# Two mixer blocks on one core: other places where the mixers' generators yield, other step rates, and another machine model in the scheduler

## The chip, the cores and the metric

The kernel runs on one core of a Trainium2 chip. The core has a matrix engine (TensorE, PE in the profile, with its weight loads shown apart as PEld), VectorE (DVE), ScalarE (ACT), GpSimd (POOL) and SyncE (SP), which here only issues transfers. The metric is the device time of one execution in microseconds (us), the median of three runs. PE's granted clock is given as a share of full speed: 1.00 is 2.4 GHz, 0.50 is 1.2 GHz.

## The reference

The input is `x` of 1024 tokens by 1024 features, in 32-bit floats. Two blocks follow one another.

```python
# first block (16 meta tokens stand in front of x)
proj = h @ w_in
y_a = hgrn2_mixer(q, f, i, g, ...)       # chunked linear attention with forget gates, 6 heads of 64
y_b = mamba2_mixer(z, xbc, dt, ...)      # convolution of 4 taps, state space scan, 6 heads, norm
y_c = s5_mixer(u, ...)                   # diagonal complex state space, gelu, then y * sigmoid(y @ glu_w + glu_b)
mixed = concatenate([y_a, y_b, y_c]) @ w_out
h = layer_norm(ALPHA * h + mixed)
h = layer_norm(ALPHA * h + square(relu(h @ w_mlp_in)) @ w_mlp_out)
...
# second block, in outline
qkv, z, beta, a, uv, gates = split(h @ w2)
y_1 = deltanet_branch(qkv, z, beta, a, ...)   # gated delta rule: a triangular inverse for each chunk, 4 heads of 128
y_2 = spatial_gating_branch(uv, ...)          # layer norm, a masked product over 128 tokens, a gate
h = layer_norm(ALPHA * h + (gated sum of y_1 and y_2, each projected) @ w_o)
h = layer_norm(ALPHA * h + conv_ffn(h))
```

## The kernel before

The tokens go through in two halves of 512. Work is of two kinds. **Dense** work is products with weights of the model: `weights` loads a block of 512 KB (tile `wr`, on SP's queue), ScalarE rounds it to the high part `wh`, VectorE subtracts for the low part `wl`, and `mm3` adds three matmuls (high by high, high by low, low by high) into PSUM tiles named `ps`. Operands (`xt`, or `f` where they come out of the mixers' tiles) are split in the same way. **Mixer** work is everything between a projection and the next one: small matmuls and transposes into PSUM tiles named `px`, with ScalarE and VectorE making the operands of the next matmul. Both pools have four banks.

A mixer is a Python generator that yields between pieces (steps). `steps`, called `st` in `run`, advances the dense generator and, after each of its steps, the mixer by `r` steps; `both` advances generators in turns. So the program's order is a mesh of the two kinds. From it the framework's scheduler makes the order of each engine: it takes the instructions by their place in the program, as its model of the machine says that they become ready. The engines then run their own orders one by one, and a waiting instruction holds up all behind it.

In `run` the stages are: the first projection `p1` with S5, HGRN2 and Mamba2 of the first half beside it; the gate of S5 (`glu`, two products of 128x512 tiles into `px`); `out_proj` of the first half and the MLP, with the second half's mixers beside them; the second block's projection `p2` for the first half and the MLP of the second half, with `mix2(0)` (delta rule for four heads, two at a time, then the spatial gating) beside them; the merge (`merge`) and `out_proj`; `p2` and the first half's FFN with `mix2(1)`; then merge, `out_proj` and FFN of the second half.

What a mixer hands on goes through DRAM: `Y1[h]` and `Y2[h]` are written by POOL's queue, read back by SP's (`load_y`: tile `ev`) and split into `xt` or `f`. In Mamba the steps' cumulative sums `m2dA` are a matmul's operand; their rows are stored to DRAM (`rows`) and come back for every chunk spread over all partitions, in two loads that ScalarE's queue issues:

```python
for c in range(c0, 5):
    ...
    for g in range(2):
        nc.scalar.dma_start(W[g][:, :, :L], rows[i:i + 3, :L]...)
        self.act(eA[g][:, :, :L], W[g][:, :, :L], AF.Exp)
```

The spatial gating ends each block of 128 tokens with four transposes (line 1175), a copy and a store to `Y2`. In the delta rule the inverse doubles its diagonal blocks: twelve small matmuls, a ScalarE copy into `Z`, matmuls on `Z`.

## Time and profile before

| | |
|---|---|
| three runs | 2838.29, 2840.65, 2842.82 us; median 2840.65 |
| span of the profiled execution | 2831.3 us |
| the median lies above that span by | 9.35 us |
| busy share of PE, weight loads, VectorE, ScalarE, GpSimd | 98, 80, 63, 41, 8% |

The profile comes from one execution. The span runs from its first to its last recorded instruction, so what lies around it (launch and end) is not in it. Times in the rows are from the span's start. A matmul's end is modelled, so "busy" counts a little more than work. Idle time in square brackets is the time in which the engine stood before the instruction, with what released it.

### The profile page before, as it was taken

The numbers are of one execution on the slowest core, as the hardware profiler recorded it, in microseconds if no ns is written. First come the engines' busy times: TensorE is split into PE (matmuls) and PEld (weight loads), VectorE is DVE, ScalarE is ACT, GpSimd is POOL, SyncE is SP. The second block draws the span as 40 slices with busy tenths as digits, with TensorE's granted clock in tenths as the row PEclk, the third lists the DMA queues.
The fourth block names the chain that finished last, engine by engine and source line by source line (L and its number), as shares of the span: only waits on it lengthen the run. The fifth ranks groups of instructions, "written<-read, shape, count | busy, mean of one in ns | idle before, by whom it ended". The sixth has DMA issues, their size and how long they took to land.

```text
span 2831.3 us, 37337 instructions
## 1 busy us (share of the span) xinstructions
PE 2768.6 (98%) x14176; PEld 2262.4 (80%) x14176; DVE 1793.7 (63%) x3321; ACT 1163.4 (41%) x1810; POOL 220.4 (8%) x365
## 2 busy tenths in 40 slices
PE   8999999999999999999999999999999999999997
PEld 7788777777878878877788888888788888888886
DVE  7678768777756554386545675535867557675556
ACT  4334344444442353364323334435545334344432
POOL 3121000000001121010000001110100000000000
PEclk9999999999999999999999999999999999999999
DMA  7333462323344444333333455433244433342232
GB/s 220 122 94 93 139 202 81 113 89 113 106 147 149 157 144 133 123 101 123 105 104 119 142 184 166 126 126 130 79 136 140 149 104 101 107 139 92 97 96 75
DMA packets 138036, 351.55 MB, mean 124 GB/s; under 512 B 26779, under 2 KB 40641, under 8 KB 137857
## 3 DMA queue, kind: packets, MB, share of 16 engines
q1 hardware_dynamic: 113712, 295.34, 32.9%
q0 software_dynamic: 16672, 48.50, 5.0%
q10 hardware_dynamic: 7473, 5.34, 0.7%
q8 instruction: 111, 1.82, 0.3%
q14 instruction: 68, 0.56, 0.1%
HBM read 296.84 MB, written 51.69 MB: 123 GB/s over the span
## 4 chain that ended last, share of the span: by engine, by line
PE 81%; issue 7%; DVE 6%; DMA 2%; ACT 2%; POOL 1%; SPq 0%; DVEq 0%; POOLq 0%; ACTq 0%
PE ps L204 73%; PE px L204 7%; DVE f L192 2%; ACT f L189 1%; DVE wl L192 1%; PE px L1265 1%; DVE f L195 1%; DMA hx<-ev 1%; DMA wr<-in_w 0%; DVE acc L195 0%; DMA f<-rows 0%; DVE f L433 0%; ACT wh L189 0%; DVE ta L192 0%; ACT ev L189 0%
## 5 line engine op out<-in xcount | busy, mean ns | idle before, releaser
L204 PE MATMUL ps<-xt,wh 128*128 128x512 f32 (+1 forms) x3616 | 1117.0, 388 | 8.7 <-ACT wh L189 8.5
L192 DVE TENSOR_TENSOR wl<-wr,wh 128x1024 fp32r<-128x1024 f32 (+3 forms) x431 | 521.5, 1210 | 606.7 <-ACT wh L189 590.2
L189 ACT ACTIVATE wh<-wr 128x1024 fp32r<-128x1024 f32 (+3 forms) x431 | 452.3, 1050 | 898.4 <-PE ps L204 826.1
L204 PE MATMUL ps<-wh,xt 128*128 128x512 f32 (+3 forms) x2624 | 813.1, 384 | 4.7 <-ACT xt L189 4.4
L204 PEld LDWEIGHTS ps<-xt,wh 128*128 128x128 f32 x3616 | 665.9, 189 | 141.7 <-ACT wh L189 8.5
L204 PE MATMUL ps<-xt,wl 128*128 128x512 f32 (+1 forms) x1808 | 698.6, 387 | 3.9 <-DVE wl L192 3.9
L204 PEld LDWEIGHTS ps<-wh,xt 128*128 128x128 f32 (+1 forms) x2624 | 485.8, 188 | 99.9 <-ACT xt L189 6.9
L204 PE MATMUL ps<-wl,xt 128*128 128x512 f32 (+3 forms) x1312 | 502.2, 383 | 0.8 <-DVE wl L192 0.7
L204 PEld LDWEIGHTS ps<-xt,wl 128*128 128x128 f32 x1808 | 341.5, 189 | 72.8 <-DVE wl L192 5.5
L204 PE MATMUL ps<-f,wh 128*128 128x512 f32 x960 | 300.5, 394 | 0.0
L204 PEld LDWEIGHTS ps<-wl,xt 128*128 128x128 f32 (+1 forms) x1312 | 246.7, 188 | 46.5 <-DVE wl L192 2.0
L189 ACT ACTIVATE f<-f 128x512 f32<-128x512 f32 (+6 forms) x300 | 178.5, 613 | 200.6 <-DVE f L192 62.3
L204 PE MATMUL px<-f,f 128*128 128x128 f32 (+8 forms) x1832 | 201.4, 258 | 16.8 <-DVE f L192 10.2
L204 PEld LDWEIGHTS ps<-f,wh 128*128 128x128 f32 x960 | 180.3, 188 | 42.3
L189 ACT ACTIVATE ev<-ps 128x512 f32<-128x512 f32 (+4 forms) x303 | 169.6, 561 | 72.9 <-PE ps L204 67.1
L192 DVE TENSOR_TENSOR acc<-acc,ps 128x512 f32<-128x512 f32 x192 | 130.8, 683 | 95.8 <-PE ps L204 93.9
L204 PE MATMUL ps<-f,wl 128*128 128x512 f32 x480 | 189.4, 394 | 0.0
L204 PEld LDWEIGHTS px<-f,f 128*128 128x128 f32 (+2 forms) x1192 | 133.3, 180 | 52.9 <-issue 22.8
L192 DVE TENSOR_TENSOR f<-f,f 128x256 f32<-128x256 f32 (+5 forms) x244 | 128.6, 547 | 39.0 <-ACT f L189 37.0
L189 ACT ACTIVATE xt<-ev 128x512 fp32r<-128x512 f32 x131 | 82.3, 629 | 149.2 <-DVE ev L192 145.9
L195 DVE SCALAR_TENSOR_TENSOR ev<-ev,p,ev 128x512 f32<-128x512 f32 x176 | 132.2, 751 | 2.7 <-ACT ev L189 0.6
L192 DVE TENSOR_TENSOR xt<-ev,xt 128x512 fp32r<-128x512 f32 x124 | 85.9, 696 | 49.6 <-ACT xt L189 49.1
(223 smaller groups left out, 2046.9 us busy)
## 6 DMA issues: line engine op xcount, KB each, us to landing
wr<-in_w SPq DMA_DIRECT2D x93, 512.0 KB, 3.8
wr<-in_wup SPq DMA_DIRECT2D x88, 512.0 KB, 3.5
wr<-in_wmi SPq DMA_DIRECT2D x64, 512.0 KB, 3.6
wr<-in_wmo SPq DMA_DIRECT2D x64, 512.0 KB, 3.6
wr<-in_wdn SPq DMA_DIRECT2D x44, 512.0 KB, 3.5
wr<-in_wo SPq DMA_DIRECT2D x32, 512.0 KB, 3.7
Y<-f POOLq DMA_DIRECT2D x32, 256.0 KB, 2.6
ev<-Y SPq DMA_DIRECT2D x32, 256.0 KB, 3.6
```

The costliest lines, as they stand in the source:

```text
L189: self.nc.scalar.activation(out=out, in_=in_, func=func, **kw)
L192: self.nc.vector.tensor_tensor(out=out, in0=a, in1=b, op=op)
L195: self.nc.vector.scalar_tensor_tensor(out=out, in0=a, scalar=s, in1=b, op0=op0, op1=op1)
L204: self.nc.tensor.matmul(out, lhsT, rhs, start=start, stop=stop)
L1265: nc.tensor.transpose(b[:, 128 * t:128 * t + 128], acc[t][:, 128 * k:128 * k + 128], self.ident)
```

## The change

Three things are changed, and no arithmetic. First, `yield`s are added or moved in the five mixers, so that a step begins with matmuls and ends with making the next operands: in HGRN2 between the operands of a level and its matmuls, in the delta rule after each copy or product that the next matmul reads, and squares are computed before the yield in front of their sums. In HGRN2 the diagonal scores move from the level of block size 1 to the first level. Second, the rates `r` in `run` rise, as the mixers now have more steps. Third, the framework is told to order the program by its other machine model (`schedule_with_timeline_sim`). Comments and docstrings are taken out as well, which shifts line numbers by some 6 to 16.

```diff
@@ -425,6 +425,7 @@
...
                     self.tt(y4[o:o + 64, :, hd, :].rearrange("p c (n b) -> p c n b", b=b), c5(M, o), c5(q, o), ALU.mult)
+                yield
                 ps = self.bank()
@@ -438,13 +439,12 @@
...
                         self.act(S[j:j + b, :, j + b:j + 2 * b], ps[j:j + b, :, j + b:j + 2 * b])
+                yield
                 scores(M, M, b, put)
-            yield
-            if b == 1:
+            if i == 0:
                 di = self.mask(M_ID)
                 scores(q, kr, 0, lambda S, ps: nc.vector.copy_predicated(out=S, mask=di, data=ps))
-        yield
@@ -457,24 +457,27 @@
...
+        yield
...
         self.act(kT, b)
-        dS = self.bank().rearrange("p (c d) -> p c d", d=64)
         if h == 0:
...
             self.act(kTm[:16], b[:16, :128])
+        yield
+        dS = self.bank().rearrange("p (c d) -> p c d", d=64)
+        if h == 0:
             for o in (0, 64):
@@ -488,19 +491,21 @@
...
         self.hs[p] = last
+        yield
         o_ = self.bank()
...
                 self.mm(o_[o:o + 64, t:t + 128], v[:, c, o:o + 64], ST[hd][:, c, :], False, True)
-        yield
...
         self.act(g, g, AF.Silu)
+        sq = self.square(o_)
+        yield
         ms = self.bank()
-        self.sums(ms, [(self.blk, self.square(o_), slice(0, 128))])
+        self.sums(ms, [(self.blk, sq, slice(0, 128))])
         r = self.t(528)[:, :512]
@@ -584,6 +589,7 @@
...
                 self.m2a.rearrange("p (o h) -> p o h", o=1).to_broadcast([128, 5 - c0, 6]), ALU.mult)
+        yield
         b = self.bank()
@@ -666,6 +672,7 @@
...
             sq.append(self.square(Y[j]))
+        yield
         ones, left, right = self.ones, self.band[:, 128:256], self.band[:, 0:128]
@@ -934,6 +941,7 @@
...
             self.act(y[j], y[j], AF.Gelu_apprx_tanh)
+        yield
         for m in range(2):
@@ -990,22 +998,23 @@
...
             self.conv4(self.S2["qkv", j, h][:, 0:515], 512, P_CWQ + 4 * j, None, x)
+        sq = [self.square(x) for x in (q, k)]
         yield
-        for x, bias in ((q, self.lnq), (k, 0.0)):
+        for x, y, bias in ((q, sq[0], self.lnq), (k, sq[1], 0.0)):
             b = self.bank()
-            self.sums(b, [(self.ones, self.square(x), slice(0, 128))])
+            self.sums(b, [(self.ones, y, slice(0, 128))])
             r = self.t(512)
...
             self.tt(x, x, r, mult)
-        yield
         E, eR = self.t(512), self.t(512)
...
+        yield
@@ -1016,8 +1025,7 @@
...
         self.act(vt, b)
-        yield
@@ -1059,6 +1067,7 @@
...
             self.act(self.halves(Z, 0, lb), nb(b))
+            yield
             b = self.bank()
@@ -1079,13 +1088,14 @@
...
             self.stt(c3(R16), c3(b), 1024.0, k1024, mult, add)
+            yield
             b = self.bank()
@@ -1098,9 +1108,11 @@
...
                 self.tt(R, vt[:, s], b[:, 0:128], sub)
+                yield
             b = self.bank()
...
             self.act(u, b[:, 0:128], AF.Copy, scale=col(be, c))
+            yield
             if S is not None:
@@ -1116,8 +1128,10 @@
...
         self.act(z, z, AF.Silu)
+        sq = self.square(o)
+        yield
         b = self.bank()
-        self.sums(b, [(self.ones, self.square(o), slice(0, 128))])
+        self.sums(b, [(self.ones, sq, slice(0, 128))])
         r = self.t(512)
@@ -1164,21 +1178,22 @@
...
             self.stt(v, v, rs, lb, ALU.mult, ALU.add)
+            yield
             b = self.bank()
...
                 self.stt(u[:, s], b[:, s], self.col(P_BS + g), u[:, s], ALU.add, ALU.mult)
+            yield
             b = self.bank()
...
                                 v.rearrange("p (g t) -> p g t", g=4))
-            yield
@@ -1485,25 +1500,25 @@
...
         m = self.both(m, self.seq(0))
-        st(p1, 3, m, 2.7)
-        st(p1, 10, m, 3)
-        st(p1, 99, m, 3, False)
+        st(p1, 3, m, 3.1)
+        st(p1, 10, m, 3.5)
+        st(p1, 99, m, 3.5, False)
         st(m)
...
         m = self.mix1(1)
-        st(self.out_proj(ys, ap["wo1"], a0), 99, m, 0.75, False)
+        st(self.out_proj(ys, ap["wo1"], a0), 99, m, 0.9, False)
         x0 = []
...
         st(n)
-        st(q, 76, m, 0.6, False)
+        st(q, 76, m, 0.72, False)
         st(m)
@@ -1514,11 +1529,11 @@
...
         st(n)
-        st(p, 99, m, 0.6, False)
+        st(p, 99, m, 1.15, False)
         q = self.mlp(x1, a1)
-        st(q, 80, m, 0.8, False)
+        st(q, 80, m, 1.5, False)
         st(m)
@@ -1531,9 +1546,9 @@
...
         st(n)
-        st(p, 99, m, 0.6, False)
+        st(p, 99, m, 1.15, False)
         q = self.ffn(0, x0, a0, ((0, 4), (4, 4), (8, 4), (12, 4), (16, 4), (20, 2)))
-        st(q, 36, m, 1, False)
+        st(q, 36, m, 1.9, False)
         st(m)
@@ -1706,7 +1721,7 @@
...
     args["out"] = nc.dram_tensor("out_0", (1024, 1024), F32, kind="ExternalOutput").ap()
-    with tile.TileContext(nc) as tc:
+    with tile.TileContext(nc, schedule_with_timeline_sim=True) as tc:
         body(tc, **args)
```

The engines' orders follow from all three together. Three places show it, all on PE.

The first is the start of Mamba's chunk loop for the first half. In the order of before, the matmuls on `m2dA` stand among dense rows of the first projection (`ps_3463`), and so do the first transposes of a chunk (L624, L633).

```order
L204 MATMUL px_3416<-m2dA_3414,o 128x30
L204 MATMUL px_3420<-o,m2dA_3414 30x128
L204 MATMUL ps_3463<-xt_119,wh_3458 128x512 x2
L624 MATMUL px_3444<-c,f_3083 16x128
L624 MATMUL px_3444<-c,f_3084 16x128
L624 MATMUL px_3444<-c,f_3085 16x128
L633 MATMUL px_3452<-c,f_3086 16x128
L204 MATMUL ps_3463<-xt_119,wl_3459 128x512
L204 MATMUL ps_3463<-xt_124,wh_3458 128x512 x2
L204 MATMUL ps_3463<-xt_124,wl_3459 128x512
L204 MATMUL ps_3463<-xt_129,wh_3458 128x512 x2
```

In the new order, the last dense rows, those of `out_proj` (`ps_4341` to `ps_4344`), are followed by the same chunk loop (L630 and L639 are its transposes there, `m2S` its state).

```order
L204 MATMUL ps_4344<-wl_4378,xt_4313 128x512
L204 MATMUL ps_4341<-wh_4377,xt_4313 128x512
L204 MATMUL ps_4342<-wh_4377,xt_4313 128x512
L204 MATMUL ps_4343<-wh_4377,xt_4313 128x512
L204 MATMUL ps_4344<-wh_4377,xt_4313 128x512
L204 MATMUL px_3598<-f_3592,f_3585 128x192 x2
L204 MATMUL px_3624<-f_3283,f_3281 128x128
L204 MATMUL px_3624<-f_3284,f_3282 128x128
L630 MATMUL px_3634<-c,f_3278 128x128
L630 MATMUL px_3634<-c,f_3279 128x128
L630 MATMUL px_3634<-c,f_3280 128x128
L639 MATMUL px_3642<-c,f_3281 128x128
```

What moved: the chunks came between the first projection's dense rows; now the dense rows stand ahead of them, and from the first of these `px` rows to the two products of `glu` there is no `ps` row.

The second place is a doubling of the delta rule's inverse in the second half (the 128x64 rows; the LDWEIGHTS rows are their operands). Before, the group `px_17546` reads what ScalarE makes of `px_17540`.

```order
L204 MATMUL px_17540<-f_17481,f_17482 128x64
L204 MATMUL ps_17653<-wl_17500,xt_17073 128x512
L204 MATMUL ps_17653<-wh_17499,xt_17073 128x512
L204 MATMUL ps_17653<-wh_17505,xt_17208 128x512
L204 LDWEIGHTS f_17482
L204 MATMUL px_17546<-f_17481,f_17482 128x64
```

In the new order the same kind of step reads as follows; `px_17454` belongs to the other head of the pair, and the group that reads what ScalarE makes of `px_17448` stands 15 rows behind this piece.

```order
L204 MATMUL px_17448<-f_17216,f_17217 128x64
L204 MATMUL ps_17659<-wh_17607,xt_17328 128x512
L204 MATMUL ps_17659<-wh_17607,xt_17445 128x512
L204 MATMUL ps_17659<-wl_17608,xt_17445 128x512
L204 MATMUL ps_17659<-wh_17607,xt_17445 128x512
L204 MATMUL ps_17707<-wh_17601,xt_17014 128x512
L204 MATMUL ps_17707<-wl_17602,xt_17014 128x512
L204 MATMUL ps_17707<-wh_17601,xt_17014 128x512
L204 MATMUL ps_17707<-wh_17601,xt_17143 128x512
L204 MATMUL ps_17707<-wl_17602,xt_17143 128x512
L204 MATMUL ps_17707<-wh_17601,xt_17143 128x512
L204 LDWEIGHTS f_17233
```

What moved: between a group and the one that depends on it there were three dense rows, and now there are seventeen, and the other head's group.

The third place is the end of the spatial gating of the second half (transposes L1175, in the new listing L1191). Before, they stand among the dense rows of the FFN.

```order
L1175 MATMUL px_18575<-c,f_18552 128x128
L204 MATMUL ps_18655<-xt_14951,wh_18651 128x512
L1175 MATMUL px_18575<-c,f_18552 128x128
L204 MATMUL ps_18655<-xt_14951,wl_18652 128x512
L1175 MATMUL px_18575<-c,f_18552 128x128
L204 MATMUL ps_18655<-xt_14959,wh_18651 128x512 x2
L204 MATMUL ps_18655<-xt_14959,wl_18652 128x512
L204 MATMUL ps_18655<-xt_14967,wh_18651 128x512 x2
L204 MATMUL ps_18655<-xt_14967,wl_18652 128x512
```

In the new order they are followed by the merge: `ps_19138`, `ps_19152` and `ps_19182` are its tiles, `f_19090` the first operand that the spatial gating gives.

```order
L204 MATMUL ps_19138<-f_19084,wh_19128 128x512
L204 MATMUL ps_19138<-f_19085,wh_19128 128x512
L204 MATMUL ps_19138<-f_19084,wl_19129 128x512
L1191 MATMUL px_18475<-c,f_18438 128x128
L204 MATMUL px_18522<-f_18483,f_18387 128x128 x2
L1191 MATMUL px_18475<-c,f_18438 128x128 x3
L204 MATMUL px_18522<-f_18483,f_18387 128x128 x2
L1191 MATMUL px_18531<-c,f_18482 128x128
L204 MATMUL px_18566<-f_18539,f_18387 128x128 x4
L1191 MATMUL px_18531<-c,f_18482 128x128 x3
L1191 MATMUL px_18575<-c,f_18538 128x128 x4
L204 MATMUL ps_19152<-f_19090,wh_19128 128x512
```

What moved: 60 us of dense rows, the FFN's, which stood between the last transposes and the merge, now stand ahead of the transposes.

## Rows read from the trace of the kernel before

**Rows 1.** The page, part 1: busy us, share of span, instructions.

```profile
PE 2768.6 (98%) x14176; PEld 2262.4 (80%) x14176; DVE 1793.7 (63%) x3321; ACT 1163.4 (41%) x1810; POOL 220.4 (8%) x365
```

**Rows 2.** By stretch: its length, busy us PE, PEld, DVE, ACT, POOL; clock; DMA.

```profile
100.00:312.00 212.00, 203.36 (x1402) 172.57 (x1401) 162.58 (x419) 86.86 (x166) 35.23 (x67) 0.98 0.33 97
312.00:419.00 107.00, 98.31 (x536) 81.98 (x534) 70.78 (x197) 43.83 (x84) 8.35 (x16) 0.95 0.59 184
...
500.00:830.00 330.00, 328.62 (x1732) 260.63 (x1731) 233.43 (x422) 145.83 (x232) 9.19 (x18) 1.00 0.34 107
...
1020.00:1360.00 340.00, 336.09 (x1936) 274.01 (x1936) 191.71 (x326) 155.06 (x266) 41.93 (x61) 1.00 0.38 123
...
1780.00:2140.00 360.00, 355.40 (x2025) 291.21 (x2025) 214.39 (x394) 168.87 (x286) 38.91 (x56) 1.00 0.35 115
```

**Rows 3.** Waits of PE's weight loads, 100:312 us: total, times, longest.

```profile
PEld px L204 <- issue: 9.9, 16, 2.9
```

**Rows 4.** The same, 500 to 830 us.

```profile
PEld px L204 <- issue: 8.6, 28, 0.9
```

**Rows 5.** The same, 1020 to 1360 us.

```profile
PEld px L204 <- ACT f L189: 8.3, 25, 1.5
```

**Rows 6.** The same, 1780 to 2140 us.

```profile
PEld px L204 <- ACT f L189: 7.3, 22, 1.6
```

**Rows 7.** Timeline, PE: start, us, operation, [idle before <-releaser]. Delta rule step.

```profile
2030.11 0.52 PE L204 MATMUL px<-f,f 128*128 128x64 f16 x12 [0.54 <-ACT f L189]
```

**Rows 8.** Timeline of PE: dense matmuls of 390 and of 512 columns.

```profile
400.54 0.34 PE L204 MATMUL ps<-wl,xt 128*128 128x390 f32 x1
...
401.09 0.34 PE L204 MATMUL ps<-wl,xt 128*128 128x390 f32 x1
...
429.32 0.39 PE L204 MATMUL ps<-wl,xt 128*128 128x512 f32 x1
...
430.01 0.39 PE L204 MATMUL ps<-wl,xt 128*128 128x512 f32 x1
```

**Rows 9.** Timeline: Mamba of the first half, its opening and its loads.

```profile
312.04 0.41 PE L204 MATMUL px<-m2dA,o 128*128 128x30 f32 x2
...
330.85 0.39 ACTq L602 DMA_DIRECT2D f<-rows  x1
...
384.53 0.52 ACT L189 ACTIVATE f<-f 128x384 f32<-128x384 f32 x1 [0.82 <-DVE f L201]
```

**Rows 10.** Transfers on the DRAM tile rows, 320 to 420 us.

```profile
  ACT f L189: 16.8, 7
...
DMA to landing us min/median/max: 2.9/4.2/5.6
```

**Rows 11.** Timeline: the gate of S5 (glu) and its output's way to PE.

```profile
420.01 3.70 PE L204 MATMUL px<-f,f 128*128 128x512 f32 x8 [0.92 <-ACT f L189]
...
425.31 0.54 POOL L947 DMA_DIRECT2D Y<-f  x1 [8.64 <-DVE f L199]
...
432.56 0.51 PE L204 MATMUL ps<-wh,xt 128*128 128x512 f32 x1 [0.53 <-ACT xt L189]
```

**Rows 12.** Timeline: the end of the last mixer stage and the merge.

```profile
2140.75 0.27 PE L1175 MATMUL px<-c,f 128*128 128x128 f32 x1
...
2141.96 0.75 POOL L1177 DMA_DIRECT2D Y<-f  x1 [2.89 <-ACT f L189]
...
2200.59 0.62 PE L204 MATMUL ps<-f,wh 128*128 128x512 f32 x2
```

**Rows 13.** The same table around the stall before 407 us.

```profile
403.00:407.00 4.00, 1.29 (x5) 0.49 (x4) 1.92 (x2) 1.65 (x3) 0.72 (x2) 0.77 0.99 390
407.00:411.00 4.00, 3.65 (x9) 2.88 (x10) 2.08 (x3) 1.97 (x4) 0.00 (x0) 0.50 0.92 255
```

**Rows 14.** VectorE's work on low parts of weights, 326 to 400 us.

```profile
L192 DVE TENSOR_TENSOR wl<-wr,wh 128x1024 fp32r<-128x1024 f32 x5 | 6.1, 1221 | 8.2 <-ACT wh L189 6.6 <-DMA f<-rows 1.6
...
L192 DVE TENSOR_TENSOR wl<-wr,wh 128x780 fp32r<-128x780 f32 x4 | 3.9, 966 | 1.7 <-ACT wh L189 1.7
```

## The prediction

> **What bounds the kernel now.** I read the page's busy shares first. PE, the matrix engine, is busy 98% of the span [rows 1], so a change that leaves the arithmetic alone can gain only what PE loses to waiting, and can lose wherever it leaves PE without work. Next came a table by stage [rows 2]. The stretches that hold mixers lose the time: PE stands idle 8.6 us of 212 in 100 to 312 us, 8.7 of 107 in 312 to 419, 1.4 in 500 to 830, 3.9 in 1020 to 1360, 4.6 in 1780 to 2140. VectorE is 77% busy in the first of these (162.6 of 212) and 56 to 71% in the others, so it doesn't bind. Then the waits. A wait can also hide behind a matmul whose end the profile models: the weight load comes late while PE still counts as busy. Those are larger, and the longest group of each stage is 9.9 us (16 times, released by nothing the profile names), 8.6, 8.3 and 7.3 us [rows 3 to 6]. The timeline shows what one looks like: twelve small matmuls of the delta rule's inverse start 0.54 us late because ScalarE has only just copied the result of the twelve before [rows 7]. That is a mixer step whose matmul follows its own producer with no dense work between.
>
> The Trainium skill, "Perfetto Trace Analysis", section "Identifying the Most-Contended Engine", says that matmul busy share is no measure of how near PE is to its peak and that the share of weight loads should be used. By the busy share of [rows 1] at most 62.7 us could be gained, by the 80% of weight loads a fifth of the span. I use neither: the sum below is priced stage by stage between PE's idle time and the late weight loads.
>
> **What the change does where mixers run beside dense work.** Counting on PE's order all matmuls of `px` tiles that have under 3 us of PE work between them and the PE instruction they depend on, there are 402 before and 92 after; in the two second-block mixer stages some 200 become none. The second place in the section on the change shows one: 3 dense rows in front of the dependent group become 17, and another head's group. So most short waits of these stages should go. Lower bound of the gain: PE's idle time alone. Upper: idle plus the longest group of late weight loads, as though none of it lay in the idle. First half's mixers up to the last cumulative sums of Mamba (100 to 312): 8.6 to 18.5, I take 15, since the remaining gaps after it are few. Second half of the first block (500 to 830): 1.4 to 10, I take 6. Second block, first half (1020 to 1360): 3.9 to 12.2, I take 7. Second block, second half (1780 to 2140): 4.6 to 11.9, I take 8. From 500 us on I take values near the middle, because not every late load is of this kind. What pays for it: the dense work beside it, which must last until the mixers end. That is where it costs.
>
> **The end of the first projection.** The matmul on `m2dA` opens the chunk loop of Mamba. Before it PE runs 534 dense matmuls of 512 columns and 120 of 390 in the old order, 720 and 214 in the new (the 264-column ones stand ahead of it in both). At 0.69 us for three of the first and 0.55 for three of the second [rows 8], 186 and 94 more are 43 + 17 = 60 us. The matmul was at 312.04 [rows 9]; now it comes at 312 + 60 - 15 = 357. Only 36 dense matmuls of `out_proj`, 8.4 us, stand behind it. Four chunks, the norms and the gate of S5 (glu) then follow one another with no dense row between, where in the old order the chunks were laced with 68 us of it. So a chain of latencies is laid bare. ScalarE issues both loads of a chunk, and its exponentials wait for them: 16.8 us in seven waits here, each load landing in 4.2 us [rows 10]. Before, the first load went out 18.8 us after `m2dA` and the last exponential ended 54.2 us after that [rows 9]. After: 17 us to the first load (ScalarE still has some 16 other operations in front, as before), 51 for five chunks of two loads (about 10 a chunk; a little less than 54.2, as ScalarE has no dense evictions in between), and 7 for the last chunk's products, gate, squares and sums. Glu then starts at 357 + 75 = 432, where it was 420.0 [rows 11]: **12 us lost**. Bounds: with the idle alone saved before it, glu is at 363 + 75 = 438 (18 lost); the other end is a rival below.
>
> Behind glu, `out_proj` wants the first of Mamba's outputs, which go through DRAM. The row of glu's own output prices that path: store issued 425.31, first matmul on it 432.56, 7.25 us [rows 11]; its norm adds a logarithm, an exponential and a product, some 2 us. Before, dense work hid it, and PE stood 0.53 us. That work has now been spent earlier; only glu's 3.7 us on PE cover it. 7.25 + 2 - 3.7 = 5.5, **5 us lost**.
>
> **The end of the last mixer stage.** In the old order the last transposes of the spatial gating run at 2140.75 and the merge that needs their outcome starts at 2200.59 [rows 12]: 60 us of dense work lie between. In the new order (third place) those transposes stand directly in front of the merge, whose second bank opens with a matmul on the gating's first tile; everything behind it on PE waits with it. The path is the same 7.25 us of [rows 11], plus a copy out of PSUM before the store (1.2 us from 2140.75 to the store's issue at 2141.96), plus two products on VectorE of about 1 us each for which the two last blocks' transposes wait, now also uncovered: **10.5 us lost**, 8 to 11. The middle stages end under cover: the same order shows dense work behind the second half's mixers (to 830) and behind 1360.
>
> **Clock.** PE was busy 1.29 us in the 4 before 407, and its granted clock was 0.50 in the next 4 [rows 13], the 1.2 GHz level; from 500 on it is 1.00 [rows 2]. Each of two long stalls (near 432 and near 2190) gives back the half speed of some 2 us of work, less what is lost today at 407: **2 us lost**.
>
> **Sum.** +12 + 5 + 10.5 + 2 - 6 - 7 - 8 = +8.5 us; the 15 us of the first stage are already in the 12. The profiled span is 2831.3 us, so about 2839.8; the median of the three runs, 2840.65, lies 9.35 above the profiled span, and I keep that: **2849 us**, 0.3% slower. Yields and rates add no work on the chip themselves: both programs hold the same matmuls, vector operations, activations and transfers.
>
> **Rivals.** *Faster.* The bare chain is not bound by the loads but by VectorE, because all loads of a chunk can be issued ahead once ScalarE is free of evictions. VectorE worked 70.8 us in 312 to 419 [rows 2], of which 10.0 were the low parts of weights [rows 14], which the new order puts ahead. That leaves at most 61 us from `m2dA` to glu: glu at 418, 2 us earlier than now; with savings at their upper ends (10 + 12.2 + 11.9) the kernel ends at 2840.65 - 2 + 5 + 10.5 + 2 - 34 = 2822. With savings as I take them, 2835. It decides at about 61 us from `m2dA` to glu. For it: the loads of before did wait behind other ScalarE work in places. Against: each load shares its queue with the exponential that frees its tile. *Same.* Losses and savings cancel, 2835 to 2846: tail 70 us or savings of 26. *Much slower.* PE has only short bursts in the bare chain. Its small matmuls there are at most 30 us (98.3 busy in 312 to 419 [rows 2], less 68 of dense work); if the clock is 1.2 GHz for all of the chain and a third to a half of them lie on it, that is +10 to +15, 2859 to 2864. For it: 0.50 in [rows 13] after one stall. Beside that row, the Trainium skill, "TensorE: Matmul & The Clock Gate", section "HAM oscillation", says that a matmul loop which waits for transfers in every pass is throttled again in every pass; no row here shows that for a long chain. *No change*, because the scheduler's new model would give the same order: excluded by the rows shown.
>
> **How the numbers follow.** My forecast (2846 to 2857) has 0.38, faster 0.26, same 0.23, much slower 0.13. About 0.2%, 5.7 us, is what a measurement of this kernel can tell from no change. Faster by more: 0.26; within: 0.23; slower: 0.51. The range takes in the much slower case, at its upper bound with the idle alone saved, 2867, and most of the faster one, to 2827.
>
> **What would show it.** In the profile after: no dense matmul between about 365 and 430 us, with PE idle some 40 us there; glu near 432; PE idle in 500 to 830, 1020 to 1360 and 1780 to 2140 near 1 us each, with fewer late weight loads; one stall of about 10 us before the merge, around 2190, and a granted clock below 1 behind both. The prediction is wrong if glu starts by 418, if no stall stands before the merge, or if the mixer stages shrink by over 30 us in all.

## The result, and the profile after

| | before | after |
|---|---|---|
| median, us (4 runs each) | 2840.22 (2838.29 to 2842.82) | 2863.93 (2862.10 to 2865.85) |
| ratio, 95% interval | | 1.0088 [1.0072, 1.0103] |

The kernel became 0.9% slower. In the profiled execution after, the time is 2865.85 and the span 2864.1, so 1.75 us lie around the span; in a second profiled execution of before it is 2838.66 and 2836.8. So under 2 us lie around a span, and most of the 9.35 us that the prediction set there came of comparing one quick execution with a median. The page after, where [rows 1] showed before:

```profile
span 2864.1 us, 37361 instructions
...
PE 2774.8 (97%) x14176; PEld 2282.8 (80%) x14176; DVE 1785.1 (62%) x3321; ACT 1162.0 (41%) x1810; POOL 221.9 (8%) x365
...
PEclk9999978999999999999999999999999999999999
```

PE's busy time rose by 6.2 us and the span by 32.8, so PE now stands idle some 27 us more. The clock row is 9 but for the sixth and seventh slices (358 to 501 us). By stretch (columns as in [rows 2]):

```profile
100.00:312.00 212.00, 212.00 (x1430) 183.42 (x1429) 148.79 (x393) 82.03 (x154) 37.55 (x71) 1.00 0.38 106
312.00:419.00 107.00, 82.08 (x464) 69.15 (x461) 72.80 (x198) 39.92 (x78) 4.85 (x9) 0.86 0.48 152
419.00:500.00 81.00, 62.86 (x253) 46.02 (x253) 53.48 (x108) 31.45 (x51) 4.62 (x9) 0.81 0.30 92
500.00:530.00 30.00, 25.85 (x129) 20.02 (x128) 18.82 (x39) 12.45 (x16) 2.65 (x5) 0.83 0.18 53
530.00:830.00 300.00, 298.73 (x1594) 238.47 (x1593) 220.68 (x408) 134.89 (x220) 7.03 (x14) 1.00 0.34 108
1020.00:1360.00 340.00, 337.00 (x1898) 279.49 (x1897) 179.46 (x285) 150.13 (x253) 39.14 (x62) 1.00 0.39 121
1780.00:2140.00 360.00, 357.75 (x2009) 296.50 (x2008) 206.50 (x359) 166.79 (x276) 34.16 (x51) 1.00 0.37 116
2140.00:2260.00 120.00, 112.01 (x523) 91.90 (x522) 80.70 (x144) 61.47 (x95) 11.23 (x10) 0.97 0.50 164
```

The same table of a second execution of before, for stretches that [rows 2] doesn't have:

```profile
419.00:500.00 81.00, 72.85 (x337) 56.71 (x338) 64.25 (x123) 37.05 (x51) 6.99 (x11) 0.92 0.32 100
500.00:530.00 30.00, 30.00 (x177) 23.78 (x176) 23.14 (x36) 11.36 (x19) 0.00 (x0) 1.00 0.38 116
530.00:830.00 300.00, 298.63 (x1556) 236.96 (x1555) 210.79 (x388) 133.81 (x212) 9.18 (x18) 1.00 0.35 108
...
2140.00:2260.00 120.00, 120.00 (x531) 97.36 (x531) 80.21 (x124) 56.75 (x80) 2.89 (x4) 1.00 0.49 156
```

In 100 to 312 us PE now has no idle time at all (212.00 of 212). In 312 to 419 it worked 98.3 us [rows 2] and works 82.1, in 419 to 500 72.9 and 62.9. From 530 to 830 nothing changed. In the second block's mixer stages PE stands idle 3.0 and 2.3 us, where [rows 2] leave 3.9 and 4.6. Around the merge (2140 to 2260) 8 us of idle time are new. The timeline of after, at the places of [rows 9, 11, 12] (PE, ScalarE and ScalarE's queue, in order of time):

```profile
358.24 0.30 PE L204 MATMUL px<-m2dA,o 128*128 128x30 f32 x2
...
377.33 1.08 PE L204 MATMUL ps<-wh,xt 128*128 128x512 f32 x4
...
377.40 0.25 ACT L189 ACTIVATE f<-px 30x128 f32<-30x128 f32 x1
...
381.47 0.39 ACTq L608 DMA_DIRECT2D f<-rows  x1
...
388.58 2.77 PE L204 MATMUL px<-f,f 16*128 16x192 f32 x8 [10.16 <-DVE f L192]
...
420.66 0.52 ACT L189 ACTIVATE f<-f 128x384 f32<-128x384 f32 x1 [0.36 <-DVE f L201]
...
429.03 1.67 ACT L189 ACTIVATE f<-f 128x512 f32<-128x512 f32 x3 [5.64 <-DVE f L192]
...
432.74 5.69 PE L204 MATMUL px<-f,o 64*128 64x512 f32 x10 [0.56 <-ACT f L189]
...
441.66 1.15 ACT L189 ACTIVATE f<-f 128x512 f32<-128x512 f32 x2 [1.31 <-issue]
...
442.34 6.44 PE L204 MATMUL px<-f,f 128*128 128x512 f32 x8 [3.91 <-ACT f L189]
...
459.43 0.50 PE L204 MATMUL ps<-wh,xt 128*128 128x512 f32 x1 [2.33 <-ACT xt L189]
...
470.39 7.07 PE L204 MATMUL px<-f,f 128*128 128x128 f32 x32 [3.62 <-DVE f L192]
...
506.27 1.12 PE L1295 MATMUL px<-c,acc 128*128 128x128 f32 x4 [2.42 <-DVE lnm L199]
...
2232.82 1.65 PE L204 MATMUL ps<-f,wh 128*128 128x512 f32 x3 [7.24 <-ACT f L189]
```

The matmul on `m2dA` comes at 358.24, the first load at 381.47, the last exponential ends at 421.18, and glu starts at 442.34. From the last dense rows, those of `out_proj` (377.33 to 378.41), to glu there is no `ps` row, and PE stands idle 31 of 64 us. Glu's eight matmuls then take 6.44 us, where [rows 11] has 3.70. Behind glu two stalls have grown: 2.33 us before the first operands of `out_proj` (0.53 in [rows 11], 1.51 in the second execution of before) and 3.62 before a group of 128x128 `px` matmuls, which had none over 1 us. The layer norm's transposes (L1295, before L1280) wait 2.42 us and, 2.6 us later, 1.46; in the second execution of before they waited nearly as long:

```profile
473.21 1.01 PE L1280 MATMUL px<-c,acc 128*128 128x128 f32 x4 [1.22 <-ACT acc L189]
...
478.19 1.12 PE L1280 MATMUL px<-c,acc 128*128 128x128 f32 x4 [2.19 <-ACT acc L189]
```

Before the merge's second bank stands one stall of 7.24.

The late weight loads, after, of 1020 to 1360 us (columns as in [rows 3]):

```profile
PEld L204 <- issue: 5.2, 19, 0.3
PEld px L204 <- ACT f L189: 1.7, 1, 1.7
```

The group of [rows 5], 8.3 us in 25 waits, is 1.7 in one; all groups together went from 23.3 to 11.9 us there, from 22.6 to 11.8 in 1780 to 2140 and from 17.8 to 2.9 in 100 to 312. In 500 to 830 they didn't fall (16.6 and 19.4; 5.3 of the 19.4 stand at the first layer norm's transposes, and from 530 on it is 15.5 and 12.6). The group of [rows 4] now reads:

```profile
PEld px L204 <- issue: 9.0, 27, 1.7
```

Two executions of one kernel differ by up to 5 us or so in where things happen, so I compare a second pair of profiles too, spans 2836.8 and 2859.7. Landmarks are weight loads on SP's queue: the last one of the MLP's second product for the first half of the tokens (`in_wmo`), behind which the second half's mixers have ended, and the first and last of each merge (`in_wab`). Columns: queue and operation, tile and source, count, ns, first to last issue. Before, second execution:

```profile
L226 SPq DMA_DIRECT2D wr<-in_wmo x32: 327/328/334, 496.0 to 870.7; - x32
...
L226 SPq DMA_DIRECT2D wr<-in_wab x8: 327/332/333, 1579.5 to 1619.2; - x8
...
L226 SPq DMA_DIRECT2D wr<-in_wab x8: 328/333/333, 2186.2 to 2225.6; - x8
```

After, second execution:

```profile
L226 SPq DMA_DIRECT2D wr<-in_wmo x32: 327/328/449, 527.7 to 899.4; - x32
...
L226 SPq DMA_DIRECT2D wr<-in_wab x8: 328/332/333, 1600.8 to 1640.1; - x8
...
L226 SPq DMA_DIRECT2D wr<-in_wab x8: 327/332/333, 2193.2 to 2246.9; - x8
```

Glu starts at 419.82 and 438.17 in these two: +18.4 us. The last `in_wmo` load is +28.7, so 10.4 more are lost behind glu. The first merge is +21.3 (7.4 won), the second +7.0 (14.3 won), its last load +21.3 (14.3 lost), the end +22.9. Per segment the prediction had +12, 0 (5 + 1 of clock - 6), -7, -8 and +11.5. The last two are safest read together: a merge whose first weights are asked for sooner counts as won and then as lost. From the first merge to the last load of the second, both profiles have 646.1 us, net 0, where +3.5 was forecast. The first pair gives +22.3 at glu, +34.6 at the last `in_wmo`, +28.5 at the first merge (6.1 won), +16.2 and +31.2 at the second (net 2.7 lost from the first merge on) and +32.8 at the end. So both pairs have the loss in the first block.

### The profile page after: what moved, and what is told of

Its sections match the earlier page's. It is cut to its first block, busy times and chain, and to the rows that moved or that the text cites. A ratio compares the mean times of both kernels' runs of the same rounds, so it can differ in the third digit from the quotient of the medians.

```text
span 2864.1 us, 37361 instructions
## 1 busy us (share of the span) xinstructions
PE 2774.8 (97%) x14176; PEld 2282.8 (80%) x14176; DVE 1785.1 (62%) x3321; ACT 1162.0 (41%) x1810; POOL 221.9 (8%) x365
## 4 chain that ended last, share of the span: by engine, by line
PE 88%; DVE 4%; DMA 3%; ACT 3%; issue 2%; SPq 0%; DVEq 0%; ACTq 0%
PE ps L204 79%; PE px L204 8%; ACT f L189 2%; DMA f<-rows 1%; DVE f L192 1%; DVE f L195 1%; DVE acc L195 1%; DMA cx<-qkv 1%; DMA wr<-in_w 1%; PE px L1280 1%; ACT wh L189 1%; DVE wl L192 1%; DMA f<-in_xT 0%; DMA cx<-sxbc 0%; DVE f L201 0%
## 5 line engine op out<-in xcount | busy, mean ns | idle before, releaser
L204 PEld LDWEIGHTS ps<-wh,xt 128*128 128x128 f32 (+1 forms) x2624 | 485.2, 188 | 98.3 <-ACT xt L189 3.6
L204 PEld LDWEIGHTS px<-f,f 128*128 128x128 f32 (+2 forms) x1192 | 144.4, 186 | 60.5 <-issue 19.7
L192 DVE TENSOR_TENSOR f<-f,f 64x256 f32<-64x256 f32 (+5 forms) x244 | 127.3, 543 | 25.9 <-ACT f L189 24.4
L189 ACT ACTIVATE f<-px 128x256 f16<-128x256 f32 (+8 forms) x164 | 66.9, 428 | 146.6 <-PE px L204 122.7
```

The lines of the kernel that those rows point to most:

```text
L189: self.nc.scalar.activation(out=out, in_=in_, func=func, **kw)
L192: self.nc.vector.tensor_tensor(out=out, in0=a, in1=b, op=op)
L204: self.nc.tensor.matmul(out, lhsT, rhs, start=start, stop=stop)
```

## The experiments

Ratios are to runs of the kernel before that were measured together with the variant, with 95% intervals; the medians of before there were 2831.4 to 2833.2 us, some 8 us under the first one. Some expectations name times in us, set beside the 2840 us of the first measurement; their ratio is what can be compared. Of the two profiles of before, the first lies near these medians and the second some 6 us above them, most of it in the second block; so differences to the second are a little kind to the variants. Landmarks as above, us:

| kernel | ratio | `m2dA` | glu | last `in_wmo` | merge 1 | merge 2, first to last load | span |
|---|---|---|---|---|---|---|---|
| before, first profile | | 312.0 | 420.0 | 869.7 | 1577.0 | 2180.7 to 2220.1 | 2831.3 |
| before_again | | 311.8 | 419.8 | 870.7 | 1579.5 | 2186.2 to 2225.6 | 2836.8 |
| after, first profile | 1.0088 [1.0072, 1.0103] | 358.2 | 442.3 | 904.3 | 1605.5 | 2196.9 to 2251.3 | 2864.1 |
| before_flag | 1.0200 [1.0186, 1.0214] | 348.6 | 429.5 | 895.2 | 1596.0 | 2173.3 to 2273.6 | 2885.7 |
| after_noflag | 1.0055 [1.0041, 1.0069] | 335.9 | 428.8 | 884.7 | 1593.4 | 2194.8 to 2234.3 | 2845.5 |
| second_only | 0.9999 [0.9990, 1.0007] | 309.9 | 418.5 | 866.2 | 1578.3 | 2180.9 to 2220.2 | 2831.2 |
| flag_second | 1.0088 [1.0074, 1.0102] | 349.1 | 432.0 | 897.6 | 1598.8 | 2191.9 to 2245.7 | 2857.5 |
| noflag_fast | 1.0064 [1.0050, 1.0077] | 316.5 | 423.8 | 881.9 | 1590.5 | 2195.7 to 2235.0 | 2846.5 |
| rates_first | 1.0011 [1.0002, 1.0020] | 303.9 | 412.0 | 876.2 | 1584.6 | 2186.8 to 2226.2 | 2836.6 |
| after_sploads | 1.0069 [1.0055, 1.0084] | 353.8 | 430.5 | 890.2 | 1591.3 | 2183.5 to 2239.4 | 2851.8 |
| before_sploads | 1.0012 [1.0003, 1.0021] | 307.9 | 417.8 | 870.2 | 1578.2 | 2180.2 to 2219.6 | 2830.7 |
| after_hold | 1.0076 [1.0063, 1.0089] | 334.7 | 433.9 | 890.9 | 1591.4 | 2184.0 to 2238.0 | 2850.2 |
| after_hold_sp | 1.0089 [1.0075, 1.0103] | 337.7 | 438.3 | 899.1 | 1599.6 | 2192.0 to 2245.8 | 2858.0 |
| after_again | 1.0103 [1.0087, 1.0119] | 355.9 | 438.2 | 899.4 | 1600.8 | 2193.2 to 2246.9 | 2859.7 |

### Which of the three parts costs

The kernel before once more, for a second profile and the spread:

> The kernel before, unchanged, for a second profile of it. The first profile's span was 2831.3 us, 9 us under the median of the runs. If 9 us of launch and end lie around the span, the span is again within 2 us of 2831; if that one execution was quick, the span comes out near 2838, and the difference to the median is under 2 us, as it is in the kernel after (2864.1 of 2865.85).

Its span was 5.5 us longer than that of the first profile, with the same program, and 1.86 us under its own time. The first execution was a quick one, then, and what is under 5 us between two profiles isn't told apart here.

The other machine model alone, on the kernel before (the last hunk of the change):

```diff
-    with tile.TileContext(nc) as tc:
+    with tile.TileContext(nc, schedule_with_timeline_sim=True) as tc:
```

> The kernel before with the scheduler's other machine model alone; steps and rates are the old ones. Theory A (the model is what puts dense work in front of the mixers): the chunk loop of Mamba opens behind 274 us of dense work in its order as in the kernel after (277), and the last gating stands where it stands after, so the time is 2857 to 2868 us, glu starts at 435 to 450 us and there is a stall of 6 to 10 us before the last merge. Theory B (more and smaller steps let dense work in between at every hop): 2833 to 2843 us, glu near 420.

Slower by 2.0%, more than the whole change and more than theory A gave it, whose direction it has; glu, at 429.5, is earlier than theory A said. Its landmarks:

```profile
L226 SPq DMA_DIRECT2D wr<-in_wmo x32: 327/328/449, 517.2 to 895.2; - x32
...
L226 SPq DMA_DIRECT2D wr<-in_wab x8: 328/332/333, 1596.0 to 1636.4; - x8
...
L226 SPq DMA_DIRECT2D wr<-in_wab x8: 327/332/333, 2173.3 to 2273.6; - x8
```

and its windows around the merge:

```profile
2140.00:2260.00 120.00, 95.15 (x488) 74.22 (x487) 67.57 (x134) 45.57 (x78) 8.65 (x10) 0.84 0.36 114
```

First block: +24.5 us to the last `in_wmo`. The second block's first half: 8.0 won (6.5 against the first profile of before). Then the merge: its first load goes out 29.4 us sooner against the first merge, and its eight loads last 100.3 us, where before has 39.4; PE stands 25 us of 120, at a clock of 0.84. So this model by itself moves dense work forward and leaves bare both the end of Mamba and the end of the last mixer stage.

The new steps and rates without the model (the whole change less that line):

> The kernel after with the scheduler's old model: new steps and rates alone. Theory A: no bare tail, since the chunk loop opens behind 237 us of dense work (217 before, 277 after); the short waits behind a step's own producer go in the mixer stages, 2820 to 2836 us. Theory B: 2852 to 2866 us, with glu behind 432.

Slower by 0.55%, so theory A, a gain, has fallen; theory B's size fits (1.004 to 1.009 as a ratio), but glu, at 428.8, is earlier than it said. The first block costs 14.0 us to the last `in_wmo`, the first half of the second block gives nothing (708.7 us between its landmarks, 708.8 before), the second 5.3 (2.3 against the first profile of before), and no stall stands before the merge (its loads last 39.5 us, and PE is busy 120.00 of the 120 us from 2140 to 2260). The chunk loop isn't bare here: `ps` rows keep PE busy 11.6 us in 390 to 410, 14.0 in the first profile of before and none in the kernel after. So these 14 us have another cause, which stays open.

The new steps and rates of the second block alone, old model (the hunks of the delta rule and the spatial gating, and the rates of the second block's mixer stages; two of the four lines are shown):

```diff
-        st(p, 99, m, 0.6, False)
+        st(p, 99, m, 1.15, False)
...
-        st(q, 36, m, 1, False)
+        st(q, 36, m, 1.9, False)
```

> The kernel before with the new steps and rates of the second block alone (delta rule, spatial gating), old model. Theory A: the gains that the profile after shows in the two second-block mixer stages, 7.7 and 8.9 us, come from the steps: 2822 to 2832 us. Theory B, or if the model alone brought those gains: 2836 to 2843 us.

No change. Between the last `in_wmo` and the first merge lie 712.1 us, where before has 708.8 (707.3 in its first profile); up to the second merge 602.6, where before has 606.7 (603.7). The late weight loads did fall, from 25.1 us in the second profile of before to 17.7 in 1020 to 1360, and the time didn't follow. The gain of after in the first of these (701.4; 701.2 in its first profile) needs the model.

Both again, the model with the new second block:

> The other machine model, with the new steps and rates of the second block only; first block's steps and rates old. With the model alone the stall complex before the last merge cost 46 us, with model and all new steps 12. Theory A (the model makes the bare tails; finer steps of the second block let its chain start earlier in the order and so shorten the last one): 46 becomes about 12, everything else as with the model alone, ratio to before 1.005 to 1.010. Rival (the first block's steps or chance did it): the 46 stay, ratio 1.016 to 1.021.

As slow as the whole change, as theory A said. The merge's loads last 53.8 us, where the model with the old steps had 100.3: the new steps of the second block repair most of what the model breaks there. The first block is like that of the model alone (897.6, there 895.2) and like that of the whole change (899.4). So the new steps and rates of the first block neither help nor hurt much once the model is on.

### Why the first block loses

Old model, new steps, first-block rates raised further, so that the mixers end early in the projection again (the second block as before):

```diff
-        st(p1, 3, m, 3.1)
-        st(p1, 10, m, 3.5)
-        st(p1, 99, m, 3.5, False)
+        st(p1, 3, m, 3.4)
+        st(p1, 10, m, 3.9)
+        st(p1, 99, m, 4.2, False)
```

> Old model, old second block, new steps of the first block, and rates of the first projection raised further, to 3.4, 3.9 and 4.2 steps (3.1, 3.5, 3.5 in the kernel after). The chunk loop then opens behind 220 us of dense work (217 before, 237 with the new rates). Theory R (the 12 us that the new steps and rates lose in the first tail without the new model come from mixers that are stepped too late, more steps at too low a rate): ratio to before 0.998 to 1.002. Rival (the finer steps themselves cost it): 1.003 to 1.006.

`m2dA` is back at 316.5 and glu at 423.8, yet the last `in_wmo` stays at 881.9, 11 us late, and the ratio at 1.0064. Theory R has fallen: in that order 4 of the 11 us lie before glu and 7 behind it, so where the chunks start is not the cause.

The rates of the change alone, on the kernel before (the same three lines, 2.7 to 3.1, 3 to 3.5 and 3 to 3.5):

> The kernel before with the first projection's rates alone raised to those of after (3.1, 3.5, 3.5); steps and model old. The chunk loop opens behind 212 us of dense work and glu behind 278 of it (217 and 286 before). If the end of the mixers' chain decides this stage, 2 to 8 us are gained, ratio 0.997 to 0.9995. If PE's short waits decide it, earlier mixers mean more of them: 1.000 to 1.003.

Glu starts at 412.0, 8 us earlier, and nothing is won: its eight matmuls take 6.70 us behind a wait of 5.12, and the last `in_wmo` comes 5.5 us later. Here an earlier glu was worth nothing; that the work behind it wasn't ready is a reading, not shown.

The chunk loads of Mamba on SP's queue, in the kernel after:

```diff
-                nc.scalar.dma_start(W[g][:, :, :L], rows[i:i + 3, :L]...)
+                nc.sync.dma_start(W[g][:, :, :L], rows[i:i + 3, :L]...)
```

> The kernel after, with the loads of Mamba's chunks issued by SyncE's queue in place of ScalarE's. Theory L (the bare chain is long because each load stands behind exponentials in ScalarE's queue): the 40 us from the first load to the last exponential become 25 to 32, ratio to before 1.004 to 1.007. Rival M (the chain is made of its ends, 23 us to the first load and 21 from the last exponential to glu, and of the hops over VectorE and PE): under 4 us change, ratio 1.008 to 1.011.

The loads on the tile `rows` in after, and then in this kernel; the second line of each is what ScalarE waited for them (us, times):

```profile
L608 ACTq DMA_DIRECT2D f<-rows x10: 326/327/393, 381.5 to 415.8; - x10
...
  ACT f L189: 19.2, 10
```

```profile
L608 SPq DMA_DIRECT2D f<-rows x10: 319/343/479, 376.8 to 401.1; - x10
...
  ACT f L189: 1.3, 1
```

The ten loads go out in 24.3 us where they took 34.3, ScalarE waits 1.3 us for them where it waited 19.2, and glu starts at 430.5. From `m2dA` to glu the chain takes 76.7 us where it took 84.1 and 82.3. So loads that queue behind ScalarE's exponentials do set part of the bare chain, 6 to 7 us of it in these traces. The ratio fell from 1.0088 or 1.0103 (two measurements) to 1.0069: a gain of 0.2 to 0.3%, at the edge of what the intervals tell. In the kernel before the same edit gains nothing (1.0012); there the chunks are laced with dense work:

> The kernel before with the loads of Mamba's chunks on SyncE's queue and nothing else. There the chunks had dense work beside them: theory A expects no change, ratio 0.998 to 1.001. If the loads were a bound of their own before the change too, 5 us or more are gained, ratio under 0.998.

To put dense work back behind `m2dA`, the weights of the projection's last six units and of the first part of its last block are held until the mixer before them has a result (a copy of one column into the weights' tile, so that the load has to wait). The lines that set `held` around those units, and `hold` to the newest result of Mamba's convolutions and sums, are left out here:

```diff
+        if self.held and self.hold is not None:
+            self.nc.vector.tensor_copy(raw[:, 0:1], self.hold)
         self.nc.sync.dma_start(raw[:, :w], src)
```

> The kernel after, new model and new steps, but the weights of the first projection's last six units and of its last block are loaded only when the mixer step before them in the program has made its result, so that this dense work (50 us) is still to be done when Mamba's chunks run: the chunk loop opens behind 227 us of dense work in place of 277. Theory A (the loss is the tail that has no dense work beside it, because the model spent that work in front of the mixers): glu starts at 418 to 432 us in place of 442, most of the 33 us that stood lost behind it come back, ratio to before 0.996 to 1.002. Rival (the mixers' chain is slow for itself under the new model, through the order on VectorE and ScalarE): PE idles earlier instead, ratio 1.006 to 1.012.

This was to decide between two readings of the first block: that the chain only lacks cover, or that the mixers themselves run late. Some 50 us of dense rows left the front of `m2dA` (PE is busy on `ps` rows 236 us up to it, 291 in after, 233 in before), but it came only 23.5 us earlier (334.7). Windows and timeline of this kernel:

```profile
300.00:320.00 20.00, 14.55 (x81) 10.49 (x82) 16.99 (x65) 5.27 (x12) 0.00 (x0) 0.53 0.30 80
320.00:340.00 20.00, 8.11 (x39) 6.74 (x38) 17.32 (x38) 6.57 (x11) 0.54 (x1) 0.54 0.46 147
```

```profile
333.69 1.20 PE L205 MATMUL px<-ta,ta 128*128 128x130 f32 x4 [9.28 <-DVE ta L193]
...
433.89 5.51 PE L205 MATMUL px<-f,f 128*128 128x512 f32 x8 [5.24 <-ACT f L190]
```

PE now waits before `m2dA`: it is busy 14.55 and 8.11 us of 20, at little over half the clock (0.53 and 0.54), while VectorE works 17.0 and 17.3; the longest wait is 9.28 us on a `ta` that VectorE makes. Glu comes only 4 to 8 us earlier. The first reading in its strong form, for which the kernel should have come back to the time of before, has fallen: VectorE's part of the mixers is behind by then. (The held loads leave PE bare in that stretch, a cost that the edit brings with it.) Where VectorE lost time, the waits of VectorE in 100 to 312 us show (engine, tile and line that waits, releaser: us in all, times, longest). After, and then before:

```profile
DVE ta L192 <- PE px L204: 20.3, 6, 5.5
```

```profile
DVE ta L192 <- PE px L204: 3.2, 5, 1.3
```

VectorE stood 20.3 us for results of small matmuls on PE, 3.2 before, and did 148.8 us of work where it did 162.6 [rows 2]. In after_hold the same wait is 20.4 us. With more dense rows in front of a mixer's matmul, PE doesn't wait, but the mixer does. In after the dense rows alone hold `m2dA` back, as PE has no idle time before it (busy 258.20 us of the 258.20 from 100 on); with 50 us of them gone it is still 22.7 us later than in before, and that rest is the mixers' lag, with what half the clock adds between 300 and 335. The division rests on this one kernel, and that VectorE's wait makes the lag is argued from its size, not shown.

With both edits:

> The same with the loads of Mamba's chunks issued by SyncE's queue as well. With dense work beside the chunks, theory A says the chain of loads is covered, so the change of queue gives less than the 5 to 12 us that it gave to the bare tail: under 4 us against after_hold. If it gives as much as there, the tail is still bare.

As slow as the whole change (1.0089, glu 438.3): the two small gains don't add up, which fits neither reading cleanly and stays open. Last, the kernel after once more, as the second profile:

> The kernel after, unchanged, beside more runs of the kernel before, because the profiles of the experiments lie 12 to 13 us under its first one and the ratios only 3 to 5. If its ratio to before is again 1.007 to 1.0095, the dense work held back won nothing that can be measured and the loads on SyncE's queue about 5 us: what delays the mixers is not the dense work in front of them alone. If it is 1.010 to 1.013, as the difference of the two first profiles would have it (32.8 us), holding the dense work back won 8 us or more and the loads 10 or more, and the bare tail is the larger part of the loss.

It came at 1.0103 [1.0087, 1.0119], on the border of the two, where the first measurement had 1.0088. Against these two, after_hold wins 0.1 to 0.3% and after_sploads 0.2 to 0.3%: small parts of the 0.9 to 1.0% that the change costs.

## Why the prediction was right or wrong

**Right**: that it is slower, and by which mechanism: dense work spent early, which leaves bare the chunk loop at the end of the first projection and the gating in front of the merge. `m2dA` was forecast at 357 and came at 358.24 and 355.9. The merge was to lose 10.5 and 1 of clock around one stall; it has one of 7.24, and its loads last 14.3 us longer. The first mixer stage of the second block was to win 7 and won 7.4 and 6.1 in the two pairs, and its late weight loads fell as forecast; the second one and the merge together were to lose 3.5 and lost 0 and 2.7. In sum the second block, with the end, gave -5.8 and -1.8 where -3.5 was forecast. PE's idle time in these two mixer stages fell to 3.0 and 2.3 us, not to the 1 that the prediction named as a sign.

**Too small** was the loss of the first block: 12 + 5 + 1 - 6 = 12 forecast, 28.7 in the second pair of profiles and 34.6 in the first. So the whole change cost 23.7 us, where 8.5 were forecast. The time, 2863.9, lies inside the range to 2867, but outside the forecast's own 2846 to 2857 and at the upper end of the rival "much slower". That it lies there is in part luck: that rival has the clock at 1.2 GHz for all of the chain, and here it was there in parts of it only, while other terms were short too. (The range's 2867 doesn't follow from its terms either: 2864 and the 6 us of "the idle alone saved" make 2870.)

The first step that failed is "17 us to the first load, 51 for five chunks, 7 for the last chunk's products": 75 us forecast, 84.1 measured, as 23.2 + 39.7 + 21.2 (82.3 in the second execution). The loads were cheaper than priced. The opening was dearer: ScalarE copied the product on `m2dA` only at 377.40, 19 us after the matmul. The closing was dearest: 8 us pass from the last exponential (421.18) to the squares (429.03), and the last of the ten matmuls of the sums (432.74) ends at 438.4. Then glu waits 3.91 us for S5's gelu, which stands on ScalarE behind the norms' activations (441.66), which "7 for the last chunk's products, gate, squares and sums" left out.

The second miss is "half-1: I take 6". From 530 to 830 us PE is idle 1.3 us with the new order and 1.4 without, and the late weight loads of [rows 4] are as many as before (9.0 us in 27). The step took them for mixer steps that the new order would cover; it doesn't. The third is "5 us lost behind glu": stalls over 1 us behind glu, up to 530 us, sum to 4.9 in the second profile of before and 11.1 in that of after, so 6.2 more (7.4 in the first pair). The sum is near the 5, but the place isn't: `out_proj`'s first operand cost only 2.33, and the largest, 3.62, is a group of mixer matmuls that waits for VectorE. Glu's own eight matmuls add 2.6 (6.27 for 3.70). Together these 8.8 us are most of the 10.4 lost behind glu.

**The clock**, 2 us forecast, is larger, and no run here prices it as a whole. One operation prices itself: glu's eight matmuls, the same in both programs, took 6.44 us where they took 3.70; the granted clock was 0.58 from 442.34 to 449, and 1.00 from 420 to 424 before. Windows of after in the bare chain:

```profile
389.00:400.00 11.00, 8.32 (x36) 6.88 (x35) 4.86 (x17) 3.36 (x8) 0.00 (x0) 0.50 0.19 48
...
405.00:410.00 5.00, 4.25 (x21) 3.92 (x22) 4.05 (x15) 2.14 (x6) 0.00 (x0) 0.50 0.27 83
...
423.00:450.00 27.00, 19.59 (x56) 10.66 (x57) 12.39 (x22) 12.70 (x22) 1.62 (x3) 0.62 0.41 117
```

PE came out of the 10.16 us wait at 0.50, the 1.2 GHz level, and was there again from 405 to 410 and partly from 423 to 450. Half speed of 8.32 and 4.25 us of work and 0.38 of 19.59 is 14 us in these stretches, an estimate, but part of it lies in time in which PE would have waited. The Trainium skill, "TensorE: Matmul & The Clock Gate", section "HAM oscillation", describes a matmul loop that is throttled again in every pass as it waits for transfers; the trace agrees in kind, 0.50 after the long wait and again later, with 0.84 to 1.00 from 400 to 405 and from 410 to 423, though here most waits are for VectorE (24.6 of PE's 31.2 us in the chain).

**A gain that came and was worth nothing**: the 15 us that PE was to win in the first stage. PE's idle time did vanish (212.00 of 212), and `m2dA`, behind 60 us more of dense rows, is 46 us later; but the work done there was work taken from the next stretch, where PE then stood. The Trainium skill, "Perfetto Trace Analysis", section "Identifying the Most-Contended Engine", says to optimize the most contended engine first, the one with the highest occupancy, and to judge TensorE by MFU (the share of its peak rate that is used) and the busy share of its weight loads. Here that engine was filled to the last in this stretch, its weight loads rose from 172.6 to 183.4 us of 212, and the kernel lost.

**Also misread** was what brings the gains. I put them down to the steps. The runs put the first one on the model: the second block's steps alone give 0.9999, the model alone 8.0 us in the same stage where the whole change wins 7.4. The new steps serve to mend the merge under that model.

**Open**: why the model orders so (its durations were not compared with the chip's); why finer steps in the first block cost 11 to 14 us without it, with the chunks covered (noflag_fast, after_noflag); why putting dense work back (after_hold) won so little; and how much of the bare chain is clock.

## What to carry to other kernels

Where an engine runs its list in order, count for each long chain at a stage's end how much independent work stands behind its first operation before and after, and price the chain as latencies without cover; that gave place and sign here, and most of the size was missing at the chain's end and behind it. Idle time that vanishes in one stage is a gain only if the stage's last result comes sooner, so look at the arrival of that result, and at who else stands waiting (VectorE 20.3 us). Try the parts of such a change one by one: the model alone cost 2.0%, the steps alone 0 to 0.6%, and together they cost 0.9 to 1.0%. Cover alone didn't mend it: with 50 us of dense work put back the kernel still lost 0.8%.

## What was not expected of the hardware

One program's profiled spans differ by 5.5 us (2831.3 and 2836.8) with the same order, so under 0.2% a single pair of traces says little. Behind a wait of 10.16 us the granted clock was 0.50 for the next 11 us of the trace, although PE was busy 8.32 of them. Ten broadcast loads went out on SP's queue in 24.3 us and on ScalarE's, between its exponentials, in 34.3.
